# Output projection and MLP of a two-layer decoder trunk in seven half-size products per 1024-cubed stage instead of eight

## The chip, the cores and the metric

One core of one Trainium2 chip runs the whole kernel. The metric is the device time of one execution in microseconds; lower is better. A core has TensorE (PE: matmuls; its weight loads are listed apart as PEld), VectorE (DVE), ScalarE (ACT), GpSimd (POOL) and SyncE (SP), which here issues the DMA transfers. Each engine works through its own instructions in order and waits on semaphores for the others.

## What is computed

Two decoder layers over 1024 tokens of width 1024, in float32. Only the end of a layer matters here:

```python
for l in range(DEPTH):                       # DEPTH = 2
    h = rmsnorm(x, norm_mix_g[l])
    ...                                      # h @ w_in, three mixers (gMLP, Mamba-2 SSD, attention)
    mix = jnp.concatenate([y_a, y_b, y_c], axis=-1)          # 1024 wide
    x = x + mix @ w_out[l]                                   # 1024 x 1024 x 1024
    x = x + squared_relu_mlp(rmsnorm(x, norm_mlp_g[l]), mlp_w1[l], mlp_w2[l])
return rmsnorm(x, final_norm_g)

def squared_relu_mlp(h, w1, w2):             # w1: 1024 x 4096, w2: 4096 x 1024
    return jnp.square(jax.nn.relu(h @ w1)) @ w2

def rmsnorm(x, g):
    var = jnp.mean(x * x, axis=-1, keepdims=True)
    return x * lax.rsqrt(var + EPS) * g
```

So a layer has nine products of 1024x1024x1024: one output projection, four for `w1`, four for `w2`.

## The kernel before

Activations lie feature-major: a tile has 128 features on the partitions and the 1024 tokens along the row. Every operand of a matmul is split in two fp32r parts, hi and lo, and a product is made as hi x hi, hi x lo and lo x hi: three matmuls of 128x128 weights against 128x512 data for each block, summed in PSUM. `split` (L108) does it: ScalarE casts hi from the source, VectorE subtracts hi from the source to get lo.

Weights come tile by tile in the fixed order of the list `specs` (L155). `fetch` issues the 512 KB load into one of RAW = 2 buffers `raw`; `prefetch` splits it into `whi` and `wlo`; `weights(n, ahead)` hands tiles out. Working tiles of 128x1024 come from a pool of N_G = 29 (`G`), large ones from a pool of two (`BIG`); PSUM has eight banks in three groups `a`, `b`, `c` of 4, 2 and 2.

After the attention a layer does this (L996 to L1056):

- *Output projection* (`wo`): for each of eight output tiles m, 48 matmuls over the eight tiles of `mix` (already split when they were written: `mAhi`/`mAlo` in `mix_a`, `mhi`/`mlo` in `p_v`), then two additions of 128x512 from PSUM into `xt[m]`. `norm_in` scales the tile by the norm's gain and splits it into `hT` at once; the factor 1/rms of a token is left out there. The squares are summed on GpSimd (`sq_add`).
- *The norm's factor*: ones-matmuls over the sums of squares (`pss`), 12 small operations on VectorE (`rstd`), and matmuls that spread the result over the partitions (`rb`, `row_bcast`). It is applied only behind the relu (`up_post`, L859), since relu lets a positive factor pass.
- *MLP* in groups of GRP = 2 hidden tiles: two `up` tiles of 48 matmuls (`feat`), relu and factor on VectorE, square and cast on ScalarE, lo on VectorE; then 96 `dn` matmuls that multiply the two hidden tiles of the group before by their part of `w2` and add into all eight `xt`, 16 additions of 128x512 on VectorE. There are 16 such groups in a layer.
- *End*: in the first layer the last group of `dn` makes the next layer's input and starts its first products (`z_start`); in the second `finish` (L873) runs the last two groups over three column ranges (FINAL) so that the final norm of one overlaps the matmuls of the next.

The code is recorded in this order; a scheduler then sets each engine's order from it and from a model of times of its own.

Of the kernel before, what the change touches and what calls it, by code (L numbers as in the profile page):

```python
# [25 lines left out]
NFF = D_FF // P  # L26
GRP = 2
SQ_EARLY = 2
W_OUT_UNIT = 42
WARM = 12  # L30
FINAL = ((0, 512), (512, 768), (768, 1024))
# [13 lines left out]
N_G = 29  # L45
RAW = 2
# [11 lines left out]
MAGIC = 0x5F3759DF  # L58


@with_exitstack
def trunk(ctx, tc, x, w_zdk, w_uv, w_f, w_q, w_kv, w_out, w1, w2, gains, pcol, prow, w_s, cst, out):
# [91 lines left out]

    specs = []  # L155
    for l in range(DEPTH):
        for i in range(4):
            specs.append((w_zdk[l, i], 2 * W_ZDK))
        for i in CONV:
            specs.append((w_f[l, i], 1024))  # L160
        for i in range(4):
            specs.append((w_uv[l, i], 1024))
        for i in (8, 9, 5, 6, 7):
            specs.append((w_f[l, i], 1024))
        for i in range(2):
            specs.append((w_kv[l, i], 768))
        for i in range(2):
            specs.append((w_q[l, i], 3 * 288))
        for i in range(8):
            specs.append((w_out[l, i], 1024))  # L170
        for g in range(NFF // GRP):
            for i in range(GRP):
                specs.append((w1[l, g * GRP + i], 1024))
            if g > 0:
                for i in range(GRP):
                    specs.append((w2[l, (g - 1) * GRP + i], 1024))
        for i in range(GRP):
            specs.append((w2[l, NFF - GRP + i], 1024))
# [32 lines left out]
    def norm_in(xm, m, gi, hT):  # L211
        hi, lo = (hsl(h, m, 0, S) for h in hT)
        g = gcol[:, gi, m:m + 1]
        act.activation(hi, xm, AF.Copy, scale=g)
        stt(lo, xm, g, f(hi), ALU.mult, ALU.subtract)
# [54 lines left out]
    def begin(l):  # L270
# [3 lines left out]
        L.sq = []  # L274
        L.dk = small.tile([P, NT, 38], F32, tag="dk", name="dk", bufs=1)
# [8 lines left out]

    def z_rest(L):
        L.yb = [G(F32, "yb") for _ in range(3)]
        for t in range(4, NT):
            L.zo.append(PA("zps"))
            for k in range(KD):
                z_mm(L, L.zo[t], t, k)  # L290
            if t == 4:
                L.r = sq_rstd(L.sq, "n")
                ts(L.rh, L.r, 0.5, ALU.mult)
            if t == 5:
                for i in range(4):
# [402 lines left out]
    def attention(L):  # L698
# [66 lines left out]
        def p_v(h, g, b0, phi, plo):  # L765
# [16 lines left out]
            if g % 2 == 1 and b0 + 2 == nk:  # L782
                if g == 1 and i == 0:
                    L.mixC[h // 2] = (G(F32R, "mhi"), G(F32R, "mlo"))
                cols = slice((g // 2) * 512, (g // 2) * 512 + 512)
                mhi, mlo = L.mixC[h // 2]
                split(mhi[rows, cols], mlo[rows, cols], avs.pop((h, g // 2))[rows, :])
# [34 lines left out]
        for n, (h, qt) in enumerate(units):  # L822
# [11 lines left out]
            if n == W_OUT_UNIT:  # L834
                prefetch(taken[0] + 1)
# [6 lines left out]
    def mix_a(L):  # L842
# [3 lines left out]
        for k in range(5):  # L846
            hi, lo = G(F32R, "mAhi"), G(F32R, "mAlo")
            for half in range(2):
# [5 lines left out]
                split(hi[:, sl], lo[:, sl], pt)  # L854
                yield
            yab[k] = None
            L.mixA.append((hi, lo))

    def up_post(o2, rrow):  # L859
        r = G(F32, "relu")  # L860
        hi, lo = G(F32R, "hhi"), G(F32R, "hlo")
        for n in range(2):
            ns = slice(n * 512, (n + 1) * 512)
            stt(r[:, ns], o2[n], 0.0, rrow[:, ns], ALU.max, ALU.mult)
        act.activation(r, r, AF.Square)  # L865
        split(hi, lo, r)
        return hi, lo

    def mlp_up(hT, rrow, ahead):
        (w,) = weights(1, ahead)  # L870
        return up_post(feat(hT, w, "up"), rrow)

    def finish(xt, cur, w2s):  # L873
        rbs = BIG(F32, "rbs")
        ob = BIG(F32, "ob").rearrange("p (m t) -> p m t", m=KD)
        od = out.rearrange("(m p) t -> p m t", p=P)

        def close(acc, a, b):
            r = sq_rstd(acc, "f", a // P, b // P)
            yield  # L880
            o = bank("c", "rb")
            for t in range((b - a) // P):
                mm(o[:, t * P:(t + 1) * P], r[:, t:t + 1].broadcast_to([P, P]), ident, True, True)
            rb = rbs[:, a:b]
            act.copy(rb, o[:, 0:b - a])  # L885
            yield
            w = 4 if b < S else 2
            for m in range(KD):
                if b < S or m % 4 == 3:
                    tt(ob[:, m, a:b], ob[:, m, a:b], rb, ALU.mult, pool)  # L890
                else:
                    stt(ob[:, m, a:b], xt[m][:, a:b], gcol[:, 4, m:m + 1], o[:, 0:b - a], ALU.mult, ALU.mult)
                if m % w == w - 1:
                    nc.sync.dma_start(out=od[:, m - w + 1:m + 1, a:b], in_=ob[:, m - w + 1:m + 1, a:b])
                if m % 2 == 1:
                    yield

        todo = iter(())
        for a, b in FINAL:
            acc = []  # L900
            for m in range(KD):
                o = bank("aab"[m % 3], "dn")
                cols_mm((o,), len(cur), lambda k: tuple(q[:, m * P:(m + 1) * P] for q in w2s[k]), lambda k: cur[k],
                        ((a, b),))
                tt(xt[m][:, a:b], o[:, 0:b - a], xt[m][:, a:b], ALU.add)
                sq = G(F32, "sq")
                act.activation(sq[:, a:b], xt[m][:, a:b], AF.Square, scale=1.0 / 32.0)
                if m == 0:
                    acc.append(sq)
                else:  # L910
                    tt(acc[0][:, a:b], acc[0][:, a:b], sq[:, a:b], ALU.add)
                if b < S or m % 4 == 3:
                    act.activation(ob[:, m, a:b], xt[m][:, a:b], AF.Copy, scale=gcol[:, 4, m:m + 1])
                next(todo, None)
            for _ in todo:
                pass
            todo = close(acc, a, b)
        for _ in todo:
            pass

    NG = NFF // GRP
# [24 lines left out]
    for l in range(DEPTH):  # L946
# [49 lines left out]
        mix = L.mixA + L.mixC  # L996
        L.mixA = L.mixC = None

        xt, sq = [], []
        hT = (BIG(F32R, "hThi"), BIG(F32R, "hTlo"))  # L1000
        for m in range(KD):
            (w,) = weights(1, 1)
            xt.append(G(F32, "x"))
            nc.sync.dma_start(out=xt[m], in_=xsrc[m * P:(m + 1) * P, :])
            os = [PA("wo") for _ in range(2)]
            cols_mm(os, KD, lambda k: tuple(q[:, k * P:(k + 1) * P] for q in w), lambda k: mix[k], HALVES)
            for o, (a, b) in zip(os, HALVES):
                tt(xt[m][:, a:b], o, xt[m][:, a:b], ALU.add)
            norm_in(xt[m], m, 2 * l + 1, hT)
            if m < SQ_EARLY:  # L1010
                sq_add(sq, xt[m], m)
        del mix, w
        for m in range(SQ_EARLY, KD):
            sq_add(sq, xt[m], m)

        (w,) = weights(1, 1)
        o0 = feat(hT, w, "up")
        r2 = sq_rstd(sq, "m")
        (w,) = weights(1, 2)
# [107 lines left out]
```

## Time and profile before

| what | value |
|---|---|
| three runs | 2407.71, 2407.99 and 2408.24 us; median 2407.99 |
| span of the profiled execution, first to last instruction | 2405.4 us |
| PE busy | 2375.9 us, 11804 matmuls |
| VectorE, ScalarE, GpSimd busy | 1338.8, 790.8, 363.2 us |
| mean granted clock of TensorE | 0.996 |

The span is that of one profiled execution; the runs without a profile lie 2.6 us above it. A matmul's end is modelled, so a row's length for a run of matmuls is read from start to start. "Idle before" is the time for which an engine waited ahead of an operation, with the instruction that ended the wait. The chain of waits is followed back from the last instruction to what released each step.

### The profile page before, as it was taken

The numbers are of one execution on the slowest core, as the hardware profiler recorded it, in microseconds if no ns is written. First come the engines' busy times: TensorE is split into PE (matmuls) and PEld (weight loads), VectorE is DVE, ScalarE is ACT, GpSimd is POOL, SyncE is SP. The second block draws the span as 40 slices with busy tenths as digits, with TensorE's granted clock in tenths as the row PEclk, the third lists the DMA queues.
The fourth block names the chain that finished last, engine by engine and source line by source line (L and its number), as shares of the span: only waits on it lengthen the run. The fifth ranks groups of instructions, "written<-read, shape, count | busy, mean of one in ns | idle before, by whom it ended". The sixth has DMA issues, their size and how long they took to land. (4 is left out here: it accounts for less than half of the span.)

```text
span 2405.4 us, 29394 instructions
## 1 busy us (share of the span) xinstructions
PE 2375.9 (99%) x11804; PEld 2014.4 (84%) x11804; DVE 1338.8 (56%) x2320; ACT 790.8 (33%) x1413; POOL 363.2 (15%) x302
## 2 busy tenths in 40 slices
PE   8999999999999999999999999999999999999997
PEld 8888899888888888888888889988888888888886
DVE  6777786345345344453667868863434434445346
ACT  5362675232121121121344537743212112112123
POOL 3052374020000000000111523722000000000002
PEclk9999999999999999999999999999999999999998
DMA  4211001211111111111222110022211111111111
GB/s 158 69 49 46 19 1 36 96 62 62 35 44 62 35 62 44 44 62 35 99 72 64 60 37 10 1 76 74 70 35 45 61 38 59 44 44 62 36 44 70
DMA packets 38599, 127.82 MB, mean 53 GB/s; under 512 B 4448, under 2 KB 6592, under 8 KB 38464
## 3 DMA queue, kind: packets, MB, share of 16 engines
q1 hardware_dynamic: 38464, 125.95, 16.0%
q8 instruction: 93, 1.52, 0.3%
q14 instruction: 42, 0.34, 0.0%
HBM read 117.50 MB, written 8.44 MB: 52 GB/s over the span
## 5 line engine op out<-in xcount | busy, mean ns | idle before, releaser
L94 DVE TENSOR_TENSOR x<-dn,x 128x512 f32<-128x512 f32 (+1 forms) x504 | 320.4, 675 | 186.7 <-PE dn L113 186.3
L865 ACT ACTIVATE relu<-relu 128x1024 f32<-128x1024 f32 x64 | 67.9, 1061 | 907.8 <-DVE relu L97 907.8
L97 DVE SCALAR_TENSOR_TENSOR relu<-up,rb 128x512 f32<-128x512 f32 x128 | 82.8, 686 | 444.8 <-PE up L113 433.1
L113 PE MATMUL dn<-hlo,whi 128*128 128x512 f32 (+1 forms) x1056 | 327.3, 384 | 0.0
L113 PE MATMUL dn<-hhi,whi 128*128 128x512 f32 (+1 forms) x1056 | 327.3, 384 | 0.0
L113 PE MATMUL dn<-hhi,wlo 128*128 128x512 f32 (+1 forms) x1056 | 326.3, 383 | 0.0
L113 PE MATMUL up<-hTlo,whi 128*128 128x512 f32 x1024 | 322.4, 393 | 0.0
L113 PE MATMUL up<-hThi,whi 128*128 128x512 f32 x1024 | 321.7, 392 | 0.0
L113 PE MATMUL up<-hThi,wlo 128*128 128x512 f32 x1024 | 319.8, 390 | 0.0
L94 DVE TENSOR_TENSOR wlo<-raw,whi 128x1024 fp32r<-128x1024 f32 (+3 forms) x188 | 234.7, 1252 | 69.6 <-ACT whi L109 41.9
L109 ACT CAST whi<-raw 128x1024 fp32r<-128x1024 f32 (+3 forms) x188 | 190.5, 1034 | 193.2 <-DMA raw<-in_w 137.7
L113 PEld LDWEIGHTS dn<-hhi,wlo 128*128 128x128 f32 x1056 | 198.7, 188 | 39.4
L113 PEld LDWEIGHTS dn<-hlo,whi 128*128 128x128 f32 x1056 | 198.7, 188 | 39.3
L113 PEld LDWEIGHTS dn<-hhi,whi 128*128 128x128 f32 x1056 | 198.7, 188 | 38.5
L113 PEld LDWEIGHTS up<-hThi,wlo 128*128 128x128 f32 x1024 | 192.2, 188 | 43.9
L113 PEld LDWEIGHTS up<-hTlo,whi 128*128 128x128 f32 x1024 | 192.3, 188 | 42.1
L113 PEld LDWEIGHTS up<-hThi,whi 128*128 128x128 f32 x1024 | 192.4, 188 | 40.5
L94 POOL TENSOR_TENSOR sq<-sq 128x1024 f32<-128x1024 f32 x24 | 63.9, 2661 | 886.1 <-ACT sq L219 885.2
L101 POOL TENSOR_SCALAR p<-p,sm 128x1024 f32<-128x1024 f32 (+6 forms) x84 | 158.1, 1890 | 125.5 <-DVE sm L743 105.8
L94 POOL TENSOR_TENSOR ob<-ob,rbs 128x256 f32<-128x256 f32 (+1 forms) x18 | 17.8, 1020 | 700.2 <-ACT rbs L885 700.2
L94 DVE TENSOR_TENSOR hlo<-relu,hhi 128x1024 fp32r<-128x1024 f32 x64 | 78.1, 1220 | 77.7 <-ACT hhi L109 77.7
L113 PE MATMUL av<-pT,vhi 128*128 128x256 f32 x480 | 115.8, 300 | 0.5 <-DVE pT L94 0.5
(232 smaller groups left out, 3749.4 us busy)
## 6 DMA issues: line engine op xcount, KB each, us to landing
raw<-in_w SPq DMA_DIRECT2D x128, 512.0 KB, 3.5
raw<-in_w_f SPq DMA_DIRECT2D x20, 512.0 KB, 3.5
x<-in_x SPq DMA_DIRECT2D x16, 512.0 KB, 4.9
raw<-in_w_out SPq DMA_DIRECT2D x16, 512.0 KB, 3.6
dec<-adr SPq DMA_DIRECT2D x16, 384.0 KB, 3.5
raw<-in_w_uv SPq DMA_DIRECT2D x8, 512.0 KB, 3.5
xd<-x SPq DMA_DIRECT2D x8, 512.0 KB, 2.6
x<-xd SPq DMA_DIRECT2D x8, 512.0 KB, 3.9
```

Of the source, the lines that this page charges most:

```text
L94: (eng or dve).tensor_tensor(out=o, in0=a, in1=b, op=op)
L97: dve.scalar_tensor_tensor(out=o, in0=a, scalar=s, in1=b, op0=op0, op1=op1)
L101: (eng or dve).tensor_scalar(out=o, in0=a, scalar1=s1, scalar2=None, op0=op0)
L109: act.copy(hi, src)
L113: pe.matmul(o, lhsT=l, rhs=r, start=start, stop=stop)
L865: act.activation(r, r, AF.Square)
```

## The change

Each of the nine products of a layer becomes a *stage* of class `Stage`: the weight matrix, the input and the output are cut into 2x2 blocks of 512x512, and the output's four blocks are made from seven block products instead of eight (Strassen's method in Winograd's form). A block product p in 1..7 is 2 halves of the contraction (kh) x 4 output tiles (j) x 2 x 3 = 48 matmuls of 128x512, into four banks. Products 5, 6, 3 and 7 use a sum or difference of weight blocks (`ssum`, or in place in `raw`; GpSimd), products 5, 6, 7 and 4 one of input blocks (`tsum`, VectorE). Products 6, 3 and 7 go on summing in the banks of an earlier product that has been read out by then. `LATE1` and `EARLY1` are the orders of the seven; `LOADS` says which raw weight blocks each fetches, so that a stage loads 18 tiles of 512 KB where it loaded 8. Both operands are split when a product is prepared (`prep_w`, `prep_b`), AHEAD = 2 half products before use; `mix` and the hidden values are kept as plain float32 instead.

`add_to` adds a product into one or two blocks of `xt`; `relu_to` copies a partial block out of PSUM on ScalarE, adds the rest and clamps it on VectorE (one custom operation), and squares on ScalarE. The MLP norm's factor is now multiplied into the input `hB` itself (`norm_half`, one half of the tokens at a time). RAW is 4, N_G 32.

```diff
+LOADS = {1: ((0, 0),), 2: ((0, 1),), 3: ((0, 1),), 4: ((1, 1),), 5: ((1, 0), (1, 1)), 6: ((0, 0),), 7: ((0, 0), (1, 0))}
+LATE1 = (1, 5, 6, 3, 7, 2, 4)
+EARLY1 = (1, 2, 5, 6, 3, 7, 4)
+SETS = ("aaaa", "bbcc")
+AHEAD = 2
...
-            hi, lo = G(F32R, "mAhi"), G(F32R, "mAlo")
+            mk = G(F32, "mixA")
...
-                split(hi[:, sl], lo[:, sl], pt)
+                act.copy(mk[:, sl], pt)
...
+        def prep_w(self, p, kh):
+            raw = {ab: take_raw() for ab in LOADS[p]}
+            if p == 5:
+                self.s[kh] = G(F32, "ssum")
+                tt(self.s[kh], raw[1, 0], raw[1, 1], ALU.add, pool)
+                v = self.s[kh]
+            elif p == 6:
+                v = self.s[kh]
+                tt(v, v, raw[0, 0], ALU.subtract, pool)
+            elif p == 3:
+                v = self.s[kh]
+                tt(v, raw[0, 1], v, ALU.subtract, pool)
+            elif p == 7:
+                v = raw[0, 0]
+                tt(v, v, raw[1, 0], ALU.subtract, pool)
+            else:
+                v = raw[LOADS[p][0]]
+            hi, lo = G(F32R, "whi"), G(F32R, "wlo")
+            split(hi, lo, v)
+            return hi, lo
...
+        for i in range(len(steps)):
+            while len(ready) < min(i + 1 + AHEAD, len(steps)):
+                st, p, kh, _ = steps[len(ready)]
+                ready.append((st.prep_w(p, kh), st.prep_b(p, kh)))
...
+            for j in range(4):
+                for kk in range(2):
...
+                    for n, (w, b) in enumerate(((wh, bh), (wh, bl), (wl, bh))):
+                        pe.matmul(os[j], lhsT=w[:, cw], rhs=b[:, cb], start=first and n == 0, stop=last and n == 2,
+                                  skip_group_check=True)
...
+        at = {1: ((0, 0),), 5: ((1, 1),), 6: ((0, 1),), 3: ((0, 1),), 7: ((1, 1), (1, 0)), 2: ((0, 0),), 4: ((1, 0),)}
...
+                    v = xt[a * 4 + j][:, half(n ^ flip)]
+                    tt(v, os[j], v, ALU.add)
...
+                if full:
+                    d = v(*full, j)
+                    dve._custom_dve(TENSOR_ADD_SAT, out=d, in0=os[j], in1=d, s0=BIGGEST, s1=0.0)
+                if keep:
+                    act.copy(v(*keep, j), os[j])
...
+        def norm_half(n, t1, t2):
+            r = sq_rstd(acc[n], "m", n * 4, n * 4 + 4, t1)
+            o = bank(t2, "rb")
+            half_bcast(r, o)
+            rb = G(F32, "rb")
+            act.copy(rb[:, 0:512], o)
             for m in range(KD):
+                stt(hB[0][:, m, half(n)], xt[m][:, half(n)], gcol[:, 2 * l + 1, m:m + 1], rb[:, 0:512], ALU.mult, ALU.mult)
...
+        stages = [Stage(mix_half, LATE1, add_to(xt, True, after_mix), True)]
+        for q in range(NQ):
+            stages.append(Stage(halves_of(LazyB()), EARLY1 if q == 0 else LATE1, relu_to(Lazy())))
+            stages.append(Stage(halves_of(Lazy()), LATE1, add_to(xt, False, (finish if last else to_next) if q == NQ - 1 else None)))
+        run(stages)
```

The order of the engines, first VectorE in the middle of an MLP. Before, in the first layer's first groups (`relu` is the hidden tile, `hlo` its lo part, `wlo` a weight tile's):

```order
L97 SCALAR_TENSOR_TENSOR relu<-up,rb 128x512 x2
L94 TENSOR_TENSOR hlo<-relu,hhi 128x1024
L97 SCALAR_TENSOR_TENSOR relu<-up,rb 128x512 x2
L94 TENSOR_TENSOR hlo<-relu,hhi 128x1024
L94 TENSOR_TENSOR wlo<-raw,whi 128x1024
```

Now, in an adding stage (`st` is a bank of a product, `blo` the lo part of an input operand):

```order
L99 TENSOR_TENSOR blo<-tsum,bhi 128x1024
L99 TENSOR_TENSOR tsum<-hid,tsum 128x1024
L99 TENSOR_TENSOR wlo<-ssum,whi 128x1024
L99 TENSOR_TENSOR tsum<-hid 128x1024
L99 TENSOR_TENSOR x<-st,x 128x512
L99 TENSOR_TENSOR blo<-tsum,bhi 128x1024
L99 TENSOR_TENSOR x<-st,x 128x512
L99 TENSOR_TENSOR wlo<-ssum,whi 128x1024
L99 TENSOR_TENSOR tsum<-hid,tsum 128x1024
L99 TENSOR_TENSOR x<-st,x 128x512
```

Preparation of the operands now stands between the additions, one by one, and `wlo` hangs on `ssum`, which GpSimd makes.

PE behind the output projection, where the norm's factor is made, first layer. Before, around the broadcast `rb` (`pss` stands 33 rows ahead of it):

```order
L113 MATMUL up<-hThi,whi 128x512
L113 MATMUL up<-hTlo,whi 128x512
L113 MATMUL rb<-cs,ry 128x128 x8
L113 MATMUL up<-hThi,whi 128x512
L113 MATMUL up<-hTlo,whi 128x512
L113 MATMUL up<-hThi,wlo 128x512
```

Now, for the second half of the tokens:

```order
L970 MATMUL st<-blo,whi 128x512
L970 MATMUL st<-bhi,wlo 128x512
L118 MATMUL pss<-ones,sq 128x2 x4
L118 MATMUL rb<-cs,ry 128x128 x4
L970 MATMUL st<-bhi,whi 128x512 x4
```

The 32 `up` matmuls between `pss` and `rb` are gone; `rb` follows `pss` directly, here behind 48 matmuls of the first `up` stage, for the first half of the tokens behind 24 of product 2 of the output projection, and in the last stage of the kernel behind product 7.

VectorE at the same place, before, the last of the 12 small steps and what follows:

```order
L94 TENSOR_TENSOR rt<-ry 128x8
L97 SCALAR_TENSOR_TENSOR rt<-rt,rv 128x8
L97 SCALAR_TENSOR_TENSOR ry<-rt,ry 128x8
L97 SCALAR_TENSOR_TENSOR relu<-up,rb 128x512 x2
L94 TENSOR_TENSOR hlo<-relu,hhi 128x1024
```

And now, the square sums and the first four of the 12 steps:

```order
L99 TENSOR_TENSOR sq<-sq 128x512 x4
L106 TENSOR_SCALAR rv<-pss 128x4
L106 TENSOR_SCALAR ry<-rv 128x4
L108 TENSOR_SCALAR ry<-ry 128x4
L99 TENSOR_TENSOR rt<-ry 128x4
```

Seven steps on, the last of the 12 and what follows it there:

```order
L102 SCALAR_TENSOR_TENSOR ry<-rt,ry 128x4
L102 SCALAR_TENSOR_TENSOR hB<-x,gcol,rb 128x512 x8
L99 TENSOR_TENSOR wlo<-raw,whi 128x1024
L99 TENSOR_TENSOR blo<-hB,bhi 128x1024
L99 TENSOR_TENSOR wlo<-raw,whi 128x1024
L99 TENSOR_TENSOR blo<-hB,bhi 128x1024
```

The operands of the second `up` product (the first `wlo` and `blo` here) now stand behind the eight scalings of `hB`, and these behind the steps.

## Rows read from the trace of the kernel before

**Rows 1.** Busy time of each engine, share of the span, instructions (the page).

```profile
PE 2375.9 (99%) x11804; PEld 2014.4 (84%) x11804; DVE 1338.8 (56%) x2320; ACT 790.8 (33%) x1413; POOL 363.2 (15%) x302
```

**Rows 2.** Chain that ended last, second layer: start us, us, engine, tile, line.

```profile
1599.70 78.07 PE wo L113 x344
...
1688.77 1.68 PE pss L113 x16
1690.45 7.44 PE up L113 x32
...
1747.10 21.99 PE up L113 x96
1769.09 21.81 PE dn L113 x96
```

**Rows 3.** Windows: length, busy PE, PEld, DVE, ACT, POOL; clock, DMA share, GB/s.

```profile
6.00:10.00 4.00, 3.02 (x15) 2.75 (x16) 3.27 (x3) 4.00 (x6) 0.04 (x1) 1.00 1.04 409
...
27.00:31.00 4.00, 2.87 (x14) 2.45 (x14) 4.00 (x2) 0.00 (x0) 1.99 (x1) 1.00 0.39 131
...
1500.00:1590.00 90.00, 90.00 (x704) 87.32 (x703) 78.59 (x193) 68.74 (x176) 57.19 (x30) 1.00 0.02 7
...
1700.00:2338.00 638.00, 638.00 (x2798) 525.03 (x2797) 283.74 (x375) 122.15 (x121) 0.00 (x0) 1.00 0.15 48
...
2389.00:2392.00 3.00, 0.34 (x2) 0.23 (x2) 1.57 (x4) 1.49 (x4) 2.04 (x3) 0.50 0.00 0
```

**Rows 4.** Timeline of VectorE, 1655 to 1702 us: start, length, operation, count.

```profile
1667.62 1.28 DVE L94 TENSOR_TENSOR x<-wo,x 128x512 f32<-128x512 f32 x2
...
1684.39 2.35 DVE L94 TENSOR_TENSOR wlo<-raw,whi 128x1024 fp32r<-128x1024 f32 x2
...
1691.42 0.16 DVE L101 TENSOR_SCALAR rv<-pss 128x8 f32<-128x8 f32 x1
...
1693.63 0.17 DVE L97 SCALAR_TENSOR_TENSOR ry<-rt,ry 128x8 f32<-128x8 f32 x1
```

**Rows 5.** Groups of VectorE and ScalarE: busy us, mean ns, idle before, releaser.

```profile
L94 DVE TENSOR_TENSOR x<-dn,x 128x512 f32<-128x512 f32 x488 | 313.7, 683 | 184.0 <-PE dn L113 183.8
...
L97 DVE SCALAR_TENSOR_TENSOR relu<-up,rb 128x512 f32<-128x512 f32 x128 | 82.8, 686 | 444.8 <-PE up L113 433.1 <-ACT rb L312 11.7
L94 DVE TENSOR_TENSOR hlo<-relu,hhi 128x1024 fp32r<-128x1024 f32 x64 | 78.1, 1220 | 77.7 <-ACT hhi L109 77.7
...
L109 ACT CAST whi<-raw 128x1024 fp32r<-128x1024 f32 x172 | 176.3, 1047 | 180.4 <-DMA raw<-in_w 137.7 <-PE wo L113 42.8
```

**Rows 6.** Tiles sq on GpSimd, hTlo on VectorE: ns minimum/median/maximum.

```profile
L94 POOL TENSOR_TENSOR sq<-sq x24: 2387/2420/3269, 10.0 to 1679.8; 128x1024 f32<-128x1024 f32 x24
...
L97 DVE SCALAR_TENSOR_TENSOR hTlo<-x,gcol,hThi x32: 1273/1286/3425, 6.2 to 1680.1; 128x1024 fp32r<-128x1024 f32 x32
```

**Rows 7.** Timeline, 6 to 40 us: GpSimd, VectorE, TensorE.

```profile
13.22 15.78 POOL L94 TENSOR_TENSOR sq<-sq 128x1024 f32<-128x1024 f32 x5 [0.69 <-ACT sq L219]
...
16.87 6.77 DVE L97 SCALAR_TENSOR_TENSOR hTlo<-x,gcol,hThi 128x1024 fp32r<-128x1024 f32 x2
...
26.80 0.46 PE L113 MATMUL zps<-wlo,hThi 128*128 128x422 f32 x1 [2.95 <-DVE wlo L94]
```

**Rows 8.** Timeline, 2370 to 2406 us: GpSimd, VectorE, TensorE.

```profile
2374.17 10.67 POOL L94 TENSOR_TENSOR ob<-ob,rbs 128x512 f32<-128x512 f32 x8 [691.92 <-ACT rbs L885]
...
2379.53 0.41 DVE L94 TENSOR_TENSOR x<-dn,x 128x256 f32<-128x256 f32 x1
...
2380.90 1.21 DVE L94 TENSOR_TENSOR rt<-ry 128x2 f32<-128x2 f32 x1
...
2386.98 0.68 PE L113 MATMUL rb<-cs,ry 128*128 128x128 f32 x4 [2.28 <-DVE ry L97]
```

**Rows 9.** DMA issues (the page): operation, count, KB each, us to landing.

```profile
raw<-in_w SPq DMA_DIRECT2D x128, 512.0 KB, 3.5
```

**Rows 10.** Group of VectorE in the attention's end: busy us, mean ns.

```profile
L94 DVE TENSOR_TENSOR mAlo<-mT,mAhi 128x512 fp32r<-128x512 f32 x20 | 12.8, 681 | 0.0
```

More of the change, by code (lines that the diff above doesn't have):

```diff
@@ L5 @@
 import concourse.tile as tile
+from concourse.dve_ops import TENSOR_ADD_SAT
 from concourse import mybir
@@ L44 @@
 CYCLE = "abac"
-N_G = 29
-RAW = 2
+N_G = 32
+RAW = 4
 VSPLIT = (0, 2, 3, 5)
@@ L168, in trunk @@
             specs.append((w_q[l, i], 3 * 288))
[L169 to L178, printed above, removed]
+        for w, order in mlp_weights(l):
+            for p in order:
+                for kh in range(2):
+                    for a, b in LOADS[p]:
+                        specs.append((w[a, b, kh], 1024))
     loaded = []
@@ L274, in begin @@
         L.sq = []
+        L.zt = list(range(NT)) if l == 0 else [4, 5, 6, 7, 0, 1, 2, 3]
         L.dk = small.tile([P, NT, 38], F32, tag="dk", name="dk", bufs=1)
@@ L783, in p_v @@
                 if g == 1 and i == 0:
-                    L.mixC[h // 2] = (G(F32R, "mhi"), G(F32R, "mlo"))
+                    L.mixC[h // 2] = G(F32, "mixC")
                 cols = slice((g // 2) * 512, (g // 2) * 512 + 512)
-                mhi, mlo = L.mixC[h // 2]
-                split(mhi[rows, cols], mlo[rows, cols], avs.pop((h, g // 2))[rows, :])
+                act.copy(L.mixC[h // 2][rows, cols], avs.pop((h, g // 2))[rows, :])
                 if g == 3 and i == 1:
@@ L869, in mlp_up @@
[L869 to L887, printed above, removed]
-            for m in range(KD):
-                if b < S or m % 4 == 3:
-                    tt(ob[:, m, a:b], ob[:, m, a:b], rb, ALU.mult, pool)
-                else:
[L892 to L919, printed above, removed]
@@ new lines, in halves_of, with sq_half @@
+    def halves_of(big):
+        return lambda b, n, kh: (big[:, b * 4 + kh * 2:b * 4 + kh * 2 + 2, half(n)],)
+    def sq_half(acc, xm, m, n, eng=None):
+        if m == 0 and acc:
+            act.activation(acc[0][:, half(n)], xm[:, half(n)], AF.Square, scale=1.0 / 32.0)
+            return
+        sq = G(F32, "sq")
+        act.activation(sq[:, half(n)], xm[:, half(n)], AF.Square, scale=1.0 / 32.0)
+        if m == 0:
+            acc.append(sq)
+        else:
+            tt(acc[0][:, half(n)], acc[0][:, half(n)], sq[:, half(n)], ALU.add, eng)
@@ L995, in trunk @@
         del L.att, L.kT, L.qT, L.vt
[L996 to L1011, printed above, removed]
```

309 lines of the change are left out of this document (227 added, 82 removed).

## The prediction

> **What bounds the kernel now.** First the busy times: TensorE is busy 99% of the span, VectorE 56%, GpSimd 15% [rows 1]. Then the chain that ended last: through a whole output projection and MLP it consists of matmuls alone, one group behind the other without a gap [rows 2]. Then the window of the second layer's MLP: in 638 us PE is busy for 638, VectorE for 284, GpSimd for 0, and the granted clock is 1.00 [rows 3]. So these stages are bound by the number of matmuls, and VectorE has more than half of its time free.
>
> What one matmul costs there: 96 `up` take 21.99 us, 96 `dn` 21.81, 344 `wo` 78.07 [rows 2], so 0.2270 to 0.2291 us each; I use 0.2285. A product of 1024x1024x1024 has 384 of them, 87.7 us; a layer has nine (one `wo`, four `up`, four `dn`), the kernel 18.
>
> **The sum's base.** The span is 2405.4 us; the three runs' median is 2408.0, so 2.6 us lie around the span, and I add them at the end.
>
> **What is taken away.** Seven half-size products are 7 x 48 = 336 matmuls of the same 128x512 shape, each with its own weight load as now. 48 fewer in each of 18 stages are 864, x 0.2285 = **197.4 us**. These lie on the chain, so this is the gain if nothing else comes late: 2405.4 - 197.4 = 2208.0. A stage then has 336 x 0.2285 = 76.8 us on PE, a product 11.0.
>
> **What is added on VectorE and GpSimd.** Each product needs its own hi/lo pairs of weights and input, two per half of the contraction: 28 splits of 128x1024 in a stage, and 8 input differences (`tsum`) of the same size: 36 VectorE operations with both inputs in SBUF. Two such, back to back, took 2.35 us [rows 4], so 1.17 each: 42.1 us. Results: in an adding stage (`wo`, `dn`) 32 additions 128x512 out of PSUM, 0.64 each by a pair that took 1.28 [rows 4], 20.5 us; in a relu stage (`up`) 16 add-and-clamp operations. No row shows that operation; the nearest are the same shape and ports, x<-dn at 683 ns and relu<-up at 686 [rows 5], so 0.64 as well, 10.2 us. Bounds: half of it, which would gain nothing while PE is the bound, and twice it, 10 us more in a relu stage, which makes pairs of 164, the price of rival B. VectorE alone: 62.6 us in an adding stage, 52.3 in a relu stage, of 76.8.
>
> GpSimd, idle there until now, gets 8 weight sums of 128x1024 in a stage. The same operation (`sq`) took 2387 ns at least and 2420 in the median [rows 6]: 19.4 us. These do not run beside VectorE. While five `sq` ran (15.78 us, 3.16 each), two hTlo, 1.29 us in the median, took 6.77 us together; and at the end, beside `ob` products on GpSimd, operations on 128x2 numbers that elsewhere take 0.17 us took 1.21 [rows 4, 6, 7, 8]. An addition out of PSUM in that same stretch kept its 0.41 [rows 8]. So two-input SBUF operations and GpSimd take turns; additions out of PSUM do not. The Trainium skill says the same as a rule ("SBUF — State Buffer", section "Who interferes with whom"): a VectorE instruction with two SBUF inputs and a GpSimd instruction that reads SBUF block each other for their whole length. The trace agrees, by the rows just named. By the rule the two engines' times add up; without it VectorE would need 114.9 us of a pair's 153.6, the 30 us below would fall away, and the sum would be 2274.
>
> Added up as taking turns: 62.6 + 19.4 = 82.0 us in an adding stage, 52.3 + 19.4 = 71.7 in a relu stage; a pair 153.7, against 2 x 76.8 = 153.6 of PE. That is a tie. What decides is what lies beside it. For: a waiting GpSimd sum slips in during the 0.64 us additions. Against: the sums come in four of the seven products (5, 6, 3, 7), where VectorE's 7.0 or 4.7 us of preparation, 2.6 of results and 4.8 of GpSimd make 12.1 to 14.4 us for 11.0 of PE, made up for in products 2, 4 and 1 (7.3, 9.6 to 12.1, 7.3). Operands are prepared two steps of 24 matmuls, 11 us, ahead, which carries most of a lag of about 11. I take 3 us lost per pair and per `wo` stage: 8 x 3 + 2 x 3 = **30 us**. Bounds: nothing, and 16 per pair (below).
>
> ScalarE casts 28 times, 1.05 us each [rows 5], 29 us, and in a relu stage copies and squares up to 20 more: under 50 of 77, hidden. DMA: 18 loads of 512 KB per stage instead of 8, 9.4 MB in 77 us or 122 GB/s; 409 GB/s were moved in a stretch at the start, and a load lands in 3.5 us [rows 3, 9], so hidden, with four buffers.
>
> **The norm's hand-over.** Before, the sums of squares (`pss`), the 12 small VectorE steps and the broadcast (`rb`) hide: 32 `up` matmuls stand between `pss` and `rb` [rows 2], since the factor was only needed at the relu. Now the MLP's input itself is scaled, so the first `up` products wait, and in the new order `rb` stands right behind `pss` on PE with nothing between. The 12 steps run from 1691.42 to 1693.80, 2.4 us [rows 4]. First half of the tokens: after product 7 come 8 additions (5.1), two additions of the next product and 4 square sums (3.9), all 128x512, `pss` 0.4, the steps 2.4, `rb` 0.7 [rows 8]: 12.5 us and PE has 24 matmuls, 5.5, for it; then ScalarE frees the bank (0.9), and product 4's operands stand behind 8 scalings (5.1) and a split pair (2.3), PE gets to them about 2 late. Some **10 us** lost. Second half: `pss` stands behind product 1 of `up`; then 0.4 + 2.4 + 0.7 + 0.9 for the copy, 8 scalings 5.1, and product 2's two splits, which stand behind these on VectorE, 2.3: **12 us** without work for PE. Two layers: **44 us**. Bounds: zero if PE is behind for another reason anyway (then VectorE uses the time to catch up), 60 if GpSimd's squares block the steps as at the end of the trace (1.21 instead of 0.17 us).
>
> **The last stage.** The same order stands there: `pss` and `rb` right behind product 7. 8 additions and 4 square sums (7.7), the steps 2.4, `pss` and `rb` 1.1: **11 us** without work, then products 2 and 4. After the last matmul the tail has the same members as now (2389 to 2405.4): additions, squares, `pss`, steps, `rb`, scaling, DMA. I leave it at its 16 us.
>
> **Clock.** Behind a 2.28 us stall that ended at 2386.98 the granted clock is 0.50, the lower level (1.2 GHz) [rows 3, 8]. Five stalls of 10 us may each do that. No row shows it rising again, so the price lies between nothing and a whole product at half rate, 11 us. A 2.95 us gap near the start left it at 1.00 [rows 3, 7], so I stay near the low end, 2.5 each: **12 us**.
>
> **Small terms.** Attention loses 22 operations per layer on VectorE (ten mAlo, 0.68 each [rows 10], and twelve mlo of the same number of columns), but PE is busy there throughout [rows 3]; I take 2 per layer off, **-4**; bounds 0 and -15. The layer boundary does the same z matmuls in another order: 0. The load of x now stands before the first stage: covered by attention.
>
> **Sum.** 2208.0 + 30 + 44 + 11 + 12 - 4 = 2301.0 in the span, + 2.6 = **2304 us**.
>
> **Rivals.**
> A. *All hidden*: GpSimd's sums fall beside additions, VectorE catches up in the stalls, the clock stays: 2208 + about 25 + 2.6 = 2236. For: the two-step lead; against: `rb` right behind `pss`.
> B. *VectorE and GpSimd become the bound*: the tie goes against PE as soon as VectorE also waits for ScalarE. In the trace hlo, which stands close behind its cast, was idle 77.7 us before 64 operations, 1.2 each [rows 5]. Now other work is put between, but 0.2 us at each of the 56 splits of a pair are 11 us: pair 165, 8 x 11 + 10 more on top of the floor: 2208 + 98 + 44 + 11 + 12 - 4 + 2.6 = 2372.
> C. *Slower than before*: the same wait, larger. From a pair of 170 or so the gain is gone: 197 minus the hand-overs' 63 leaves 134, or 17 per pair, 0.3 us at each split. At the 0.5 us mean, pairs of 182: 2208 + 8 x 28 + 63 + 6 = about 2500. Against: most splits have an addition or another split ahead of them in the new order, and the cast is under way by then.
>
> **Chances.** Forecast (2265 to 2335) 0.5; A 0.13; B (2335 to 2400) 0.27; C 0.10. The range reaches through A's middle and most of B: 2235 to 2385. 0.2%, 4.8 us, is about what a measurement can tell from no change: faster 0.88, same 0.02, slower 0.10.
>
> **What would show it.** PE's matmuls in a `dn`/`up` pair: 672 in 154 to 158 us, with gaps ended by VectorE's blo or wlo; if gaps are everywhere and VectorE is over 95% busy, B. GpSimd's ssum near 2.4 us if it is free, 3 or more if they take turns; two-input rows on VectorE well above 1.22 in the mean. A PE gap of 5 to 15 us before `rb`, twice a layer and once in the last stage, ended by VectorE's ry; a clock below 1.00 behind it. Wrong would be: an add-and-clamp far from 0.69 us, weights late from DMA, or matmuls no longer 0.2285 apart.

## The result and the profile after

| | before | after |
|---|---|---|
| median of four runs beside each other | 2408.1 us | 2295.4 us (2294.9 to 2296.4) |
| ratio, 95% interval | 1 | 0.9533 [0.9519, 0.9546] |
| span of the profiled execution | 2405.4 us | 2294.3 us |
| mean granted clock | 0.996 | 0.977 |

112.7 us are gained, against 104 forecast: 2295 measured, 2304 predicted, range 2235 to 2385. The total came out better than its steps did. The page of after, busy times:

```profile
PE 2203.1 (96%) x10844; PEld 1866.2 (81%) x10844; DVE 1918.2 (84%) x2572; ACT 1120.1 (49%) x1841; POOL 800.4 (35%) x444
```

There are 960 matmuls fewer, 864 by the seven products and 96 because 192 matmuls of 128x256 among the last `dn` were made of 96; VectorE is busy for 579 us more, GpSimd for 437. The chain of waits after, around the stages of both layers (start us, us, what):

```profile
445.90 10.52 PE st L970 x45
493.89 21.17 PE st L970 x92
627.21 507.58 PE st L970 x2238
1134.78 23.09 PE zps L118 x120
...
1618.70 21.15 PE st L970 x92
1752.81 439.61 PE st L970 x1938
```

From 627 us on, the first layer's stages are one row of 2238 matmuls, 0.2268 us each from start to start, without a break; before that the chain is in pieces. Windows after, first layer: the output projection's first five products and half of the sixth, up to `rb` (404 to 484), then up to the second `rb`, then the rest up to 627, and the steady part (columns: length, busy PE, PEld, DVE, ACT, POOL; clock, DMA share, GB/s):

```profile
404.00:484.00 80.00, 67.67 (x275) 54.30 (x276) 71.52 (x88) 27.20 (x36) 24.22 (x10) 0.88 0.32 105
484.00:520.00 36.00, 32.66 (x143) 26.80 (x142) 26.20 (x38) 15.77 (x23) 7.20 (x4) 0.93 0.20 59
520.00:627.00 107.00, 97.57 (x402) 78.50 (x402) 98.74 (x78) 51.47 (x59) 49.36 (x15) 0.92 0.42 134
...
627.00:1134.00 507.00, 506.80 (x2236) 419.64 (x2237) 458.83 (x412) 239.41 (x272) 158.08 (x53) 1.00 0.39 123
```

In the steady part PE is busy throughout though VectorE is at 90%. What the first layer's stages lose they lose in the first 223 us, where PE waits and the mean granted clock is 0.88 to 0.93; the second layer loses again in its last stage. PE's timeline after, its waits of over 2 us in the first layer's stages and in the last stage (start us, us, operation, count, in brackets the idle time before and what ended it):

```profile
403.88 2.08 PE L970 MATMUL st<-bhi,whi 128*128 128x512 f32 x4 [2.26 <-ACT bhi L114]
...
425.65 2.07 PE L970 MATMUL st<-bhi,whi 128*128 128x512 f32 x4 [3.69 <-ACT bhi L114]
...
479.09 1.86 PE L118 MATMUL pss<-ones,sq 128*128 128x2 f32 x8 [5.78 <-DVE sq L99]
483.38 2.08 PE L118 MATMUL rb<-cs,ry 128*128 128x128 f32 x8 [2.43 <-DVE ry L102]
...
518.28 1.16 PE L118 MATMUL rb<-cs,ry 128*128 128x128 f32 x8 [2.43 <-DVE ry L102]
522.00 2.07 PE L970 MATMUL st<-bhi,whi 128*128 128x512 f32 x4 [2.56 <-ACT bhi L114]
527.81 0.79 PE L970 MATMUL st<-blo,whi 128*128 128x512 f32 x1 [3.73 <-DVE blo L99]
...
560.77 0.80 PE L970 MATMUL st<-blo,whi 128*128 128x512 f32 x1 [3.07 <-DVE blo L99]
...
2247.65 1.87 PE L118 MATMUL pss<-ones,sq 128*128 128x2 f32 x8 [9.01 <-DVE sq L99]
2251.95 2.07 PE L118 MATMUL rb<-cs,ry 128*128 128x128 f32 x8 [2.43 <-DVE ry L102]
```

The second layer repeats the first layer's pattern (2.26 and 3.16 us at the start, 5.83 before `pss`, 2.43 before either `rb`, then 2.56, 3.73 and 2.08). Groups of VectorE after (busy us, mean ns | idle before):

```profile
L99 DVE TENSOR_TENSOR blo<-tsum,bhi 128x1024 fp32r<-128x1024 f32 x144 | 252.3, 1752 | 38.7 <-ACT bhi L114 38.7
...
L99 DVE TENSOR_TENSOR x<-st,x 128x512 f32<-128x512 f32 x320 | 208.3, 680 | 12.4 <-PE st L970 12.3
...
L1000 DVE CUSTOM_DVE_ANT_0 hid<-st,hid 128x512 f32<-128x512 f32 x128 | 83.5, 685 | 54.6 <-PE st L970 54.5
```

And the tile `ssum` on GpSimd (ns minimum/median/maximum):

```profile
L99 POOL TENSOR_TENSOR ssum<-raw x36: 2440/3300/5265, 399.1 to 2185.4; 128x1024 f32<-128x1024 f32 x36
L99 POOL TENSOR_TENSOR ssum<-ssum,raw x36: 2390/3332/3355, 413.5 to 2191.3; 128x1024 f32<-128x1024 f32 x36
L99 POOL TENSOR_TENSOR ssum<-raw,ssum x36: 2442/3362/3447, 428.1 to 2205.4; 128x1024 f32<-128x1024 f32 x36
```

The turns are there: sums of 2.4 us take 3.3 in the median, a two-input row like `blo` 1.75 in the mean instead of 1.22 (1.23 in the median, 3.46 at most: some rows are held up for a whole sum, most not at all), and additions out of PSUM keep their 0.68. So they cost VectorE time, but no steady-state PE time. What do they cost, then, and where?

For what follows, each kernel's stages are measured on PE: from the first stage's start to `zps` in the first layer (403.88 to 1134.78, where the chain has it, 730.9 us), and to the last `pss` in the second (1528.40 to 2279.47, 751.1). 3024 matmuls of 0.2268 us in each would be 685.8, so after loses 45 and 65, **110 us**. This counts everything above 0.2268 us a matmul, also waits that the kernel before has: its second layer, from the first `wo` (1585.78) to the last `pss` (2391.80), lies 22 us above 3456 such matmuls.

### The profile page after: what moved, and what is told of

It is laid out like the page before. It is cut to its first block, busy times and chain, and to the rows that moved or that the text cites. A ratio compares the mean times of both kernels' runs of the same rounds, so it can differ in the third digit from the quotient of the medians.

```text
span 2294.3 us, 28842 instructions
## 1 busy us (share of the span) xinstructions
PE 2203.1 (96%) x10844; PEld 1866.2 (81%) x10844; DVE 1918.2 (84%) x2572; ACT 1120.1 (49%) x1841; POOL 800.4 (35%) x444
## 4 chain that ended last, share of the span: by engine, by line
PE 78%; DVE 13%; issue 3%; ACT 2%; POOL 2%; DMA 2%; SPq 0%; POOLq 0%; ACTq 0%; DVEq 0%
PE st L970 45%; PE cqkv L118 5%; PE xbc L118 5%; PE uvps L118 4%; PE av L118 4%; DVE blo L99 3%; PE sc L118 3%; DVE wlo L99 3%; DVE tsum L99 2%; PE zps L118 2%; PE pTp L778 2%; PE qps L118 2%; DVE x L99 1%; POOL ssum L99 1%; DMA raw<-in_w 1%
## 5 line engine op out<-in xcount | busy, mean ns | idle before, releaser
L970 PE MATMUL st<-blo,whi 128*128 128x512 f32 x2016 | 793.9, 394 | 16.4 <-DVE blo L99 16.2
L970 PE MATMUL st<-bhi,whi 128*128 128x512 f32 x2016 | 780.7, 395 | 18.5 <-ACT bhi L114 16.5
L970 PE MATMUL st<-bhi,wlo 128*128 128x512 f32 x2016 | 791.3, 393 | 0.0
L970 PEld LDWEIGHTS st<-blo,whi 128*128 128x128 f32 x2016 | 383.6, 190 | 103.2 <-DVE blo L99 22.9
L970 PEld LDWEIGHTS st<-bhi,whi 128*128 128x128 f32 x2016 | 383.9, 191 | 102.1 <-ACT bhi L114 18.1
L970 PEld LDWEIGHTS st<-bhi,wlo 128*128 128x128 f32 x2016 | 383.0, 190 | 80.1
L114 ACT CAST bhi<-tsum 128x1024 fp32r<-128x1024 f32 x144 | 151.2, 1050 | 345.1 <-DVE tsum L99 288.4
L99 DVE TENSOR_TENSOR blo<-tsum,bhi 128x1024 fp32r<-128x1024 f32 x144 | 252.3, 1752 | 38.7 <-ACT bhi L114 38.7
L99 DVE TENSOR_TENSOR x<-st,x 128x512 f32<-128x512 f32 x320 | 208.3, 680 | 12.4 <-PE st L970 12.3
L99 DVE TENSOR_TENSOR wlo<-ssum,whi 128x1024 fp32r<-128x1024 f32 x108 | 176.5, 1634 | 7.7 <-ACT whi L114 6.8
```

The source lines that it names most:

```text
L99: (eng or dve).tensor_tensor(out=o, in0=a, in1=b, op=op)
L114: act.copy(hi, src)
L970: pe.matmul(os[j], lhsT=w[:, cw], rhs=b[:, cb], start=first and n == 0, stop=last and n == 2, skip_group_check=True)
```

## Experiments

The kernel before ran beside every experiment, and its median lay between 2408.1 and 2409.8 us. After itself did not run again beside the experiments, so a difference of 2 or 3 us between kernels of different rounds tells nothing, and one of 5 us is at the edge of what can be told.

**Is it the order on PE?** `e1_banks` gives `pss` and `rb` other banks, so that matmuls of the next product may stand ahead of them:

```diff
-                norm_half(0, "a", "b")
+                norm_half(0, "a", "a")
...
-                close(1, "a", "a", 0)
+                close(1, "b", "c", 0)
```

> Edit: the sums of squares and the broadcast of the norm's factor take other PSUM banks (first half of the tokens, and the last stage), so that the matmuls of the following product need not wait for the broadcast's bank and may run before it; 24 of them now stand ahead of pss in each layer, 55 in the last stage. Theory (PE stands still only because its next matmuls were put behind pss and rb): the stalls before pss, 5.8 us in each layer and 9.0 in the last stage, and the 2.4 us between pss and rb behind them go, 27 us, and the low clock behind them with them, some 15 us more: about 2255 us. Rival (VectorE is the one that is late there, and the operands of the product after next come late by the same amount): the gaps only move to bhi or blo of the next products, 2285 to 2296 us.

Measured: 2290.4 us, 5 less, in the rival's range. PE's timeline of `e1_banks`, the same place:

```profile
482.18 1.16 PE L118 MATMUL rb<-cs,ry 128*128 128x128 f32 x8 [2.88 <-DVE ry L102]
485.95 2.07 PE L970 MATMUL st<-bhi,whi 128*128 128x512 f32 x4 [2.62 <-ACT bhi L114]
491.76 0.79 PE L970 MATMUL st<-blo,whi 128*128 128x512 f32 x1 [3.73 <-DVE blo L99]
...
519.85 1.20 PE L970 MATMUL st<-bhi,whi 128*128 128x512 f32 x4 [2.62 <-ACT bhi L114]
525.66 0.80 PE L970 MATMUL st<-blo,whi 128*128 128x512 f32 x1 [4.61 <-DVE blo L99]
```

The 5.8 us before `pss` are gone, and 2.6 and 3.7 us stand behind `rb` instead, since the next operands wait for VectorE as before. The length of a gap at a place does not tell what that place costs.

**The factor's chain.** `e4_no_factor` leaves out `pss`, the steps, `rb` and its copy in both MLPs, so its output is another:

```diff
-            r = sq_rstd(acc[n], "m", n * 4, n * 4 + 4, t1)
-            o = bank(t2, "rb")
-            half_bcast(r, o)
-            rb = G(F32, "rb")
-            act.copy(rb[:, 0:512], o)
+            acc[n].clear()
+            rb = ones[:, 0:1].broadcast_to([P, 512])
```

> Edit: the MLP's input is scaled by the gain and by ones instead of the norm's factor; pss, the 12 steps, rb and its copy are left out in both halves of both layers (the output is then another); the square sums and the eight scalings stay, and the last stage is untouched. Theory (the hand-over's chain pss, steps, rb, copy is what PE waits for): of the 63 us of gaps the stages have, 5.8 + 2.4 + 2.4 and most of 2.6 + 3.7 go in each layer, 30 us, with 8 us of pss and rb work and some 20 us of low clock: about 2237 us. Rival (the operands queue behind the eight scalings all the same, and the clock costs little): only pss, the steps and rb go, 2 x 10: 2270 to 2280 us.

Measured: 2265.2 us, 30 less; between the two and nearer the rival. Timeline of PE in `e4_no_factor`:

```profile
485.32 0.50 PE L970 MATMUL st<-blo,whi 128*128 128x512 f32 x1 [2.82 <-DVE blo L99]
499.30 0.50 PE L970 MATMUL st<-blo,whi 128*128 128x512 f32 x1 [2.79 <-DVE blo L99]
...
530.04 1.20 PE L970 MATMUL st<-bhi,whi 128*128 128x512 f32 x4 [1.83 <-ACT bhi L114]
```

With no factor to wait for, PE still waits for VectorE's `blo`. The eight scalings and the operands still stand in VectorE's queue; what the scalings cost there was not tried apart.

**Do the sums matter, though the steady state hides them?** Both directions. `e3_sums_twice` puts a second operation of the same shape behind each sum, at all four places (it took 1.89 us at least, where a sum takes 2.39):

```diff
                 tt(v, v, raw[0, 0], ALU.subtract, pool)
+                tt(v, v, ones[:, 0:1].broadcast_to([P, 1024]), ALU.mult, pool)
```

> Edit: behind each of the 144 sums of weight blocks on GpSimd stands one more operation of the same size with two inputs (a product with ones, in place, which changes no value). Theory (VectorE's two-input operations and GpSimd take turns, and VectorE, 91% busy in the steady state with those waits in it, has some 14 us per pair of stages to spare): 16 more of 2.4 us per pair are 39 us, of which the 32 us of operations out of PSUM can hide a part, so that pairs grow by 10 to 25 us: 2295 + 8 x 10 to 25 = 2375 to 2500 us, with VectorE near 100% and PE's gaps ended by blo and wlo. Rival (the two engines do not hold each other up, or the sums slip in beside the additions): GpSimd has 66% of its time free, so nothing changes: 2290 to 2300 us.

Measured: 2476.6 us, 181 more, 1.26 us for each added operation; inside the theory's range, and slower than the kernel before the change. Window and timeline of `e3_sums_twice` where after had no gap:

```profile
700.00:1000.00 300.00, 278.71 (x1184) 226.08 (x1183) 263.54 (x199) 125.41 (x142) 174.24 (x60) 0.97 0.35 111
...
837.20 0.79 PE L974 MATMUL st<-blo,whi 128*128 128x512 f32 x1 [6.68 <-DVE blo L99]
```

GpSimd is busy for 174 us of 300 and VectorE for 264, and still PE waits 21, all of it for VectorE's `blo`: neither engine is full. VectorE is held up in two ways there. Its rows get longer (`blo<-tsum` 1.85 us in the mean), and it waits 12.4 us for the casts `whi`, which hang on sums (`ssum`) that now come later. What each of the two adds to the 181 us the run does not tell.

`e2_no_sums` leaves the sums out, so its output is another; at product 5 for instance:

```diff
-                self.s[kh] = G(F32, "ssum")
-                tt(self.s[kh], raw[1, 0], raw[1, 1], ALU.add, pool)
-                v = self.s[kh]
+                v = raw[1, 0]
```

> Edit: the 144 sums of weight blocks on GpSimd are left out, products 5, 6, 3 and 7 take one raw block each (the output is then another); loads, splits and matmuls stay. Theory (in the steady state TensorE is the bound, and what is lost in the first three stages of a layer is VectorE being late, of whose time there the turns with GpSimd take some 35 of 196 us): nothing changes between 630 and 1130 us, and each layer gains 10 to 15 us in its first three stages: 2265 to 2275 us; two-input rows on VectorE fall to about 1.22 us. Rival (the first stages are late by the chain pss, steps, rb, copy alone, not by VectorE's load): 2288 to 2297 us.

Measured: 2247.1 us, 48 less, more than the theory's 20 to 30. To see where, take the time in three parts. The time from a stage's start to its first `rb` falls from 79.5 to 64.8 us in the first layer and from 79.8 to 65.4 in the second; from the first `rb` to the second it stays (34.9 and 34.8 in the first layer); behind it, up to the end of the layer's stages, 5.6 go in the first layer, and 12.5 up to the last stage's `pss` in the second. So the sums cost 14.5 us in the first part of each output projection, and some 5 behind each hand-over; that leaves 7 for the last stage, where the wait before `pss` falls from 9.01 to 3.94. These are places where VectorE starts without a lead or has just lost it. This is worked out from the two timelines; which product loses how much was not tried apart.

**The same sums on VectorE.** `e7_sums_vector` makes them on VectorE, at all four places:

```diff
-                tt(v, v, raw[0, 0], ALU.subtract, pool)
+                tt(v, v, raw[0, 0], ALU.subtract)
```

> Edit: the 144 sums of weight blocks are made on VectorE instead of GpSimd; nothing else. Theory (the two engines take turns: a sum costs VectorE about as much while GpSimd makes it, in longer blo, wlo and tsum rows, as if it made it itself, 1.22 us): VectorE gets 176 us of sums and loses some 200 us of holding up, so the time stays: 2285 to 2302 us, with blo<-tsum back at 1.22 us. Rival (GpSimd's sums fall mostly beside operations out of PSUM and cost VectorE little): pairs of stages have 20 us more on VectorE, 96% busy becomes over 100%: 2320 to 2400 us.

Measured: 2272.3 us, 23 less, ratio to before 0.9433 [0.9419, 0.9447]; below the theory's range too, and faster than the kernels before and after; the result is the same. Page and groups of VectorE in `e7_sums_vector`:

```profile
PE 2197.0 (97%) x10844; PEld 1862.3 (82%) x10844; DVE 1849.5 (81%) x2716; ACT 1125.3 (50%) x1841; POOL 351.5 (15%) x300
...
L99 DVE TENSOR_TENSOR blo<-tsum,bhi 128x1024 fp32r<-128x1024 f32 x144 | 176.7, 1227 | 34.4 <-ACT bhi L114 27.4 <-PE st L970 6.7
...
L99 DVE TENSOR_TENSOR ssum<-raw,ssum 128x1024 f32<-128x1024 f32 x36 | 44.0, 1223 | 0.0
```

VectorE makes 144 operations more, 176 us of work, and is busy for 69 us less. A sum takes it 1.22 us; GpSimd needs 2.4 to 3.3, and a two-input row of VectorE that meets one takes up to 3.46. The Trainium skill's rule that the two block each other ("SBUF — State Buffer", section "Who interferes with whom") is borne out by `blo`, 1752 ns with the sums on GpSimd and 1227 without.

But that need not be all of the 23 us. A sum also stands on the way from the load to the cast of its operand. In after's chain between 404 and 627 us some 21 us are GpSimd's own sums, one of them:

```profile
586.67 5.28 POOL ssum L99
```

In `e7_sums_vector` some 5 us of the chain there are sums. So a shorter sum and a VectorE that is not held up go together in this run, and no run parts them. By place, the move gives back only 4 of the 14.5 us of each output projection, but nearly all of the rest (4.6 of 5.6 in the first layer, 10 of 12.5 in the second): at the start of a layer VectorE stays late with its own sums.

**Order on VectorE.** In `e5_later_banks`, `norm_half` makes only the broadcast and the scalings, and is recorded later (parts of the edit):

```diff
             elif p == 7:
-                norm_half(0, "a", "b")
+                fac[0] = sq_rstd(acc[0], "m", 0, 4, "a")
             elif p == 2:
+                norm_half(0, "b")
...
             elif p == 4:
-                norm_half(1, "a", "a")
+                fac[1] = sq_rstd(acc[1], "m", 4, 8, "a")
...
+            if hook and p == 1:
+                hook(1, "a")
```

> Edit: as e1_banks, and in both halves the broadcast of the norm's factor and the eight scalings are recorded one product later than the sums of squares and the steps, behind the operands of the product that follows (first half: behind product 2 of the output projection, second half: behind product 1 of the first up stage). Theory (at the hand-over VectorE stands idle, some 26 us in the first three stages of a layer, and puts the scalings ahead of operands that are wanted earlier; both end): the stalls before pss and behind rb shrink by 10 to 12 us per layer, and the last stage's by 5: about 2268 us. Rival (VectorE is late whatever the order, and the gaps move on as they did in e1_banks): 2283 to 2292 us.

Measured: 2281.8 us, 13.5 less, of which `e1_banks` had 5; just below the rival's range. PE's timeline of `e5_later_banks`:

```profile
493.77 1.20 PE L970 MATMUL st<-bhi,whi 128*128 128x512 f32 x4 [2.12 <-ACT bhi L114]
...
501.76 0.79 PE L970 MATMUL st<-blo,whi 128*128 128x512 f32 x1 [6.79 <-DVE blo L99]
...
517.68 2.08 PE L118 MATMUL rb<-cs,ry 128*128 128x128 f32 x8 [2.43 <-DVE ry L102]
```

Now the first `up` product's `blo` comes late, by 6.8 us, behind the first four of its matmuls. Most of the loss moved on.

> Edit: e5_later_banks and e7_sums_vector together. Theory: the later scalings give their gain as there, and without GpSimd's turns VectorE catches up a little sooner behind the hand-over, since no two-input operation takes 3.3 us there: 2258 to 2268 us. Rival (VectorE's total is what counts, and it is the same): the time of e5_later_banks within 3 us.

`e8_both`, the two together, took 2270.4 us, 0.9426 [0.9412, 0.9440]: within 2 us of `e7_sums_vector`, their ranges overlapping. With the sums on VectorE the later scalings bring nothing to speak of.

**The clock.** Around the waits the granted clock falls (0.66 in the mean of after's window below, part of it at the lower level, 1.2 GHz). `e6_busy` gives PE matmuls without use while it waits:

```diff
+    def keep_busy(o, n):
+        w, b = lastop
+        for _ in range(n):
+            pe.matmul(o, lhsT=w[:, 0:P], rhs=b[:, 0:512], start=True, stop=True, skip_group_check=True)
```

> Edit: TensorE gets matmuls to do while it waits (20 before pss of the first half, 36 before pss of the last stage, 8 between pss and rb, 16 behind the second half's rb; each repeats a block of the product just finished into a bank that is overwritten afterwards); the waits of everything else stay, and so does the result. Theory (about 59 us of stage work run at the lower clock behind the stalls, which costs 29 us): with TensorE busy through the large stalls the granted clock stays at 1.00 behind them, and pss and rb take half as long: 20 to 25 us less, 2270 to 2276 us. Rival (the clock costs what was forecast, 12 us, or less, and the time is that of the waits): 2283 to 2297 us.

Measured: 2290.2 us, 5 less, in the rival's range. One window in after, then in `e6_busy`:

```profile
471.00:484.70 13.70, 5.49 (x25) 4.67 (x24) 9.99 (x26) 2.52 (x4) 0.00 (x0) 0.66 0.08 31
```

```profile
471.00:484.70 13.70, 12.95 (x63) 10.27 (x62) 11.19 (x28) 4.33 (x7) 0.00 (x0) 1.00 0.09 35
```

And PE's timeline of `e6_busy` there:

```profile
471.79 4.83 PE L248 MATMUL pss<-bhi,whi 128*128 128x512 f32 x20 [0.43 <-DVE x L99]
...
478.26 0.95 PE L118 MATMUL pss<-ones,sq 128*128 128x2 f32 x8
...
481.65 1.16 PE L118 MATMUL rb<-cs,ry 128*128 128x128 f32 x8
...
491.83 0.50 PE L980 MATMUL st<-blo,whi 128*128 128x512 f32 x1 [2.65 <-DVE blo L99]
```

The clock holds, `pss` and `rb` take 1.0 and 1.2 us instead of 1.9 and 2.1, and PE then waits 2.65 us for `blo`, where after waits 0.34: being faster, it arrives before VectorE. The 59 us at the lower clock of the expectation were too many. Counted on the timelines, about 97 of after's stage matmuls stand about 0.43 us apart instead of 0.227, 20 us, and the slow `pss` and `rb` add about 5; in `e6_busy` about 60 are left, behind the gaps that were not filled. So some 12 us of slowness were taken away and about 5 came back as time.

Would it count for more once VectorE has room? `e9_vector_busy` fills the stalls of `e7_sums_vector` in the same way; `e10_vector_busy_banks` also moves the last stage's banks as in `e1_banks`.

> Edit: e7_sums_vector with matmuls for TensorE while it waits, as in e6_busy (8 between pss and rb, 16 behind the second half's rb, 20 before pss of the last stage; none before pss of the first half). Theory (in the changed kernel the lower clock cost only 5 us because VectorE was late in the same stretch, so that a slow TensorE waited less; with the sums on VectorE it has more room, and the low clock costs more of its face value): 8 to 15 us below e7_sums_vector: 2257 to 2264 us. Rival (the waits of the hand-over are what counts, and the clock is worth 5 us in either): 2265 to 2269 us.

> Edit: e9_vector_busy, but in the last stage pss and rb take other PSUM banks as in e1_banks, so that matmuls of the product behind may stand ahead of them (instead of the repeated ones there). Theory (the last stage's gap before pss, 5.2 us in e7_sums_vector, is then filled with work): 3 to 6 us below e9_vector_busy. Rival (its gap moves behind rb, as the layers' gaps did in e1_banks): the same as e9_vector_busy within 2 us.

Measured: 2274.9 us (2273.1 to 2275.8) and 2277.6 (2275.1 to 2279.6), neither below `e7_sums_vector`; both theories fall, and the rivals miss too (by 6 and by 0.7 us). Against `e7_sums_vector`, 2.6 us more in `e9_vector_busy` are too few to call a loss: the ratios to before are 0.9446 [0.9432, 0.9460] and 0.9433 [0.9419, 0.9447]. The mean clock rose from 0.983 to 0.988 in the first. The filling itself stands ahead of real work there, as in `e6_busy` (16 matmuls behind `rb`, 3.9 us, where PE would have gone on after 2.6), so these runs tell what filling gives, not what the clock costs. `e10_vector_busy_banks`' last stage has 2.2, 2.6 and 3.7 us around `rb`: its gap moved, as in `e1_banks`.

**Do the two losses add?** `e11_neither`:

> Edit: e2_no_sums and e4_no_factor together: neither the 144 sums of weight blocks nor the factor's chain in the two MLPs (pss, steps, rb, copy); the output is another. Theory (the sums' 48 us and the chain's 30 us are losses at different places, and add): 2295 - 78 = 2217 us, about 17 above 2200, which is the floor with matmuls 0.2268 apart (2208.0 + 2.6 - 10). Rival (both are the same loss, VectorE late at the hand-over, and taking one away leaves little of the other): 2235 to 2247 us.

Measured: 2209.9 us, 85.5 less, 7 more than 48 and 30 together. So the losses add: without the sums the factor's chain costs 37 us, and without the chain the sums cost 55. The theory of two separate losses holds, though the time lies 7 us below its 2217. Page and timeline of `e11_neither`:

```profile
PE 2170.5 (98%) x10780; PEld 1844.5 (84%) x10780; DVE 1688.8 (77%) x2524; ACT 1126.0 (51%) x1837; POOL 349.4 (16%) x300
...
405.59 1.20 PE L965 MATMUL st<-bhi,whi 128*128 128x512 f32 x4 [2.26 <-ACT bhi L114]
...
485.91 0.50 PE L965 MATMUL st<-blo,whi 128*128 128x512 f32 x1 [0.90 <-DVE blo L99]
```

These are the only two gaps of over 0.7 us in the first layer's stages. The stages' loss over 685.8 us per layer, by kernel:

| kernel | first layer, us | second, us | lost in both |
|---|---|---|---|
| after | 730.9 | 751.1 | 110 |
| `e7_sums_vector` | 722.5 | 735.9 | 87 |
| `e4_no_factor` | 714.2 | 733.2 | 76 |
| `e2_no_sums` | 710.6 | 723.5 | 63 |
| `e11_neither` | 689.5 | 702.1 | 20 |

Of the 20 left, 16 are in the second layer, where the last stage's own `pss` and `rb` remain untouched.

## Why the prediction was right, and where its steps were not

- *The matmuls taken away*: right. 48 fewer per stage are the gain. They stand 0.2268 us apart after; before, 96 `up` and 96 `dn` took 43.80 us [rows 2], 0.2281 each. So the 6048 that stay cost some 8 us less than they did, which was not foreseen; the cause is open.
- *GpSimd and VectorE take turns*: shown, by `ssum`, `blo` and `e7_sums_vector`. Rival B, where the tie goes against PE in every pair, did not come. With twice the operations on GpSimd PE does wait in the steady part (`e3_sums_twice`, 181 us more), so the margin was narrow; that run does not show B's own reason, VectorE's wait for ScalarE at every split.
- *30 us of slip, 3 in each pair and in each `wo` stage*: the step that failed. It is 0 in the steady part (PE busy for 506.80 of 507 us); that VectorE catches up in products 2, 4 and 1 and that two steps of lead carry the rest, as was reckoned, fits but was not tried. But the sums cost 48 us all the same (`e2_no_sums`): 14.5 in each output projection, the rest behind the hand-over and in the last stage. The argument "12.1 to 14.4 us for 11.0 of PE in products 5, 6, 3, 7" fits the output projection, where these come behind product 1 with no lead from a stage before; for product 7 it is too low by the prediction's own count, since 8 additions (5.1 us) follow that product and 2.6 are reckoned.
- *Norm's hand-over, 44 us*: the mechanism right, the size a little high. The gaps there are 5.78 + 2.43 us at the first half and 2.43 + 2.56 + 3.73 at the second, 17 a layer where 22 were reckoned. Leaving the chain out gave 30 us, and 37 where the sums were gone too, the clock behind it in that. The 5.78 before `pss`, which the working has as additions and square sums behind product 7, goes when the sums go (`e2_no_sums`): VectorE was late from them, not from the norm. With both away, 20 are left of 110.
- *Last stage, 11 us*: right, 9.01 + 2.43; but in `e2_no_sums` the 9.01 are 3.94, so 5 of them came from the sums, which the term's working does not have.
- *Clock, 12 us*: a cost was right, its size stays open. At face value it is about 25 us; filling the large stalls gave about 5, with filling that stands in the way itself. The lower level also follows the gaps at the output projection's start, which were not filled.
- *Add-and-clamp, 0.64 us, additions 0.64, ScalarE and DMA hidden*: right, 685 and 680 ns by mean (0.64 by start to start in pairs), and loads landing in 3.6 us.
- *Not foreseen*: the gaps at the output projection's start, 2.26 and 3.69 us in the first layer, 2.26 and 3.16 in the second. Before, some 40 of the 384 `wo` matmuls stood among the attention's last matmuls (the chain's 344 in [rows 2] are those behind); after, the first stage begins only behind all of these. The -4 for the attention cannot be read apart from this.

The total was right by luck. Without any loss the stages would have gone from 6912 matmuls of 0.2281 us to 6048 of 0.2268, a gain of 205 us. The span became 111 us shorter, so 94 were lost, and the terms 30 + 44 + 11 + 12 - 4 are 93. What was too low in one place (the start of a layer's stages) was too high in another (the steady state), and the 7 us by which the span lies below the forecast 2301 are the closer spacing. (The 110 of the table is not to be held against the 93, since it counts what the stages before lost as well.)

## What to carry to other kernels

Where two engines together stand near the time of the engine that is the bound, do not spread the expected slip evenly over the stages. Read it from the order, at the places where the helping engines have no lead (a first stage, or behind a dependency), since the steady state may hide all of it. Moving small work to an idle engine does not pay by itself: here the same sums were 23 us cheaper on the engine that seemed full, where each took half the time and no second engine stood in the way. And what a gap costs is found by taking away its cause; when only the order around it was changed, it moved on.

## What the runs showed of the hardware that was not expected

- Sums of 128x1024 cost the kernel more on GpSimd than on VectorE (2295.4 against 2272.3 us): 2.4 us alone and 3.3 in turns, against 1.22.
- The 2.26 us gap ahead of the first stage was followed by the lower level, 1.2 GHz. In after it came at once: the first four matmuls took 2.08 us, and the window from 404 to 425 us has a granted clock of 0.91 in the mean. In `e11_neither`, behind the same 2.26 us, the first four took 1.20, and the clock was at 0.51 a little later (window 407.5 to 411 us). The 2.95 us gap in [rows 7] left it at 1.00. So the length of one gap alone does not tell whether or when the lower level follows.
- Half the granted clock did not mean half the speed of the kernel: matmuls stood 0.43 us apart instead of 0.227, but in `e6_busy`, of some 12 us of slowness taken away, about 5 came back as time, as PE then waited for VectorE instead.
